# Seven places for gathered rows instead of four, and a quarter of the scratch for dynamic DMAs

## The chip, the core and the metric

The kernel runs on one core of a Trainium2 chip. The metric is the device time of one execution in microseconds (us). Before the change three runs took 2218.74, 2220.05 and 2222.28 us, with a median of 2220.05 us. The engines are named as in the profile: PE is TensorE (PEld its weight loads), DVE is VectorE, ACT is ScalarE, POOL is GpSimd, and SP is the queue that issues most plain DMAs.

## The reference, cut to what matters

Two transformer blocks run on a sequence of 512 tokens of width 1024, all in float32. The first block has attention with a sliding window, a convolution branch and a gated feed-forward layer. The second has a spatial gate, an attention over selected keys, and at its end a layer called PEER: each token picks 128 of 16,384 experts (8 heads, 16 each), and an expert is a row of two tables of 16,384 x 1024 numbers.

```python
def blk(args):                 # xb: 128 tokens, eb: 128 expert numbers of each, gb: their gates
    ub = u_tab[eb]
    vb = v_tab[eb]
    a = jax.nn.gelu(jnp.einsum('td,ted->te', xb, ub))
    return jnp.einsum('te,ted->td', (gb * a).astype(vb.dtype), vb)
```

## The kernel before

**Dense and gathered tokens.** The expert layer does most tokens densely. For the first 320 tokens PE multiplies with all 128 blocks of `peer_u` (`u_block`, 24 products of 128x320 each), and for the first 384 tokens with all 128 blocks of `peer_v` (`v_block`, 18 products of 128x512 each); what a token did not choose has weight zero. The other tokens use gathers: POOL issues an indirect DMA that fetches one row of 4 KB into each of 128 partitions (512 KB in all), and DVE multiplies. The generator `gathered()` holds the 320 gathers and their DVE instructions in this order: 64 from `peer_u` (for 64 tokens with 128 experts each, two experts of a token on two partitions; multiplied with `h[1]`, sums in `ga2`), 128 from `peer_u` (the last 128 tokens, multiplied with `h[3]`, sums in `ga`), and 128 from `peer_v` (added into `h[3]`).

**The ring.** All 320 go through one tile name with `GBUFS` buffers, which are the "places":

```python
def gather(table, idx, k):
    r = pg.tile([128, 1024], F32, name="rows", bufs=GBUFS)
    G.indirect_dma_start(out=r, out_offset=None, in_=table,
                         in_offset=bass.IndirectOffsetOnAxis(ap=idx[:, k:k + 1], axis=0))
    return r
# in gathered(), the last of its three loops:
        r = gather(A["peer_v"], gidx, k)
        with tc.issue_after(pace[0]):
            V.scalar_tensor_tensor(h[3], r, ga[:, k:k + 1], h[3], op0=OP.mult, op1=OP.add)
```

Gather k can be issued when the DVE instruction of gather k-4 has run. Weights have such rings too (`unit()`): four `raw` buffers that SP fills, and four each of `whi` (a cast by ACT, L137) and `wlo` (a subtraction by DVE, L139), which PE reads. A `raw` buffer is free again when its `wlo` has run.

**What sets the order.** Each engine runs its instructions in a fixed order. `advance(gen, us)` mixes the gathers among weight blocks by the costs that the generators yield (`G1_US`, `G_US`); a scheduler below then orders each engine's list, and `issue_after` keeps a gather's DVE instruction behind the `wlo` named by `pace`. Three stretches matter here:

- About 585 to 620 us: the norms on the way into the second block. DVE writes a scaled sum of squares, POOL turns it into `rstd` (L163), DVE scales `xs` (L174), PE transposes it. Soon after, the pool `b2g` is opened, which loads `vg`, `vb`, `wsT` and `bs` from ACT's queue (L93, L755, L760); POOL then masks `wsT` with four affine selects (L757).
- 1106 to about 1515 us: choice of experts and dense `peer_u` blocks. The first 64 gathers begin here. Where the program needs all of them (`while not made2: next(gat)`), those left over, 18 in the trace, follow each other; then ACT makes `zg` from `ga2`, PE multiplies it with `fold` (L1015), and building goes on.
- From there to the end: the 128 `v_block`s (the first product starts at 1516.9 us), with 28 of the `u_block`s among them, the other gathers, and loads of `gl` (gate weights, 1.5 MB for eight blocks) and `al` (stored `peer_u` results). A block's gate weights are multiplied by DVE (`gl`, L1164), cast by ACT (`wvhi`, L151), and split by DVE (`wvlo`, L152) before PE can start on it.

**The scratch.** [...] A place for gathered rows takes 4,096 bytes of each partition.

Of the kernel before, what the change touches and what calls it, by code (L numbers as in the profile page):

```python
# [19 lines left out]
DRAM = bass.MemoryType.DRAM  # L20
EPS = 1e-6
NEG = -1.0e30
GBUFS = 4

R_US = 2.1
TOP_US = 4.0
# [33 lines left out]
def tile_layers(ctx: ExitStack, tc: tile.TileContext, A: dict, out: bass.AP):  # L60
# [818 lines left out]
# [5 lines that stand above are left out]
# [446 lines left out]
```

## Time and profile before

| | before |
|---|---|
| median of 3 runs | 2220.05 us |
| the profiled execution, its own time | 2223.98 us |
| its span, first to last instruction | 2222.3 us |
| PE busy | 2082.0 us, 94% |
| DVE busy | 1583.9 us, 71% |
| ACT busy | 863.1 us, 39% |
| POOL busy | 501.1 us, 23% |
| moved by DMA | 476.47 MB |

The shares are means over stages with different limits. The line of GB/s in the profile shows the two halves: about 100 GB/s until 1100 us, and 290 to 373 GB/s from there until shortly before the end. [...] A wait is idle time of an engine and is put down to what ended it.

### The profile page before, as it was taken

The page shows a single profiled execution, that of the slowest core. Times are in us where ns is not written, and L with a number is a line of the kernel's source. Part 1 is how long each engine was busy: PE and PEld are TensorE (multiplying, and loading weights), DVE is VectorE, ACT ScalarE, POOL GpSimd, SP SyncE. Part 2 cuts the span into 40 slices and gives each one's busy share as a digit, 9 for nine tenths or more (in the row PEclk, how much of TensorE's full clock was granted, in tenths as well). Part 3 has the DMA queues.
Part 4 walks back from the last instruction along what each step waited for, and adds up shares of the span by engine and source line. Part 5 has one row for each costly group of instructions (what it writes and reads, how often), then busy time and mean ns, then how long its engine had stood idle before and what let it go on. Part 6 is the DMA issues. An engine that isn't in the chain of part 4 may idle for free.

```text
span 2222.3 us, 29478 instructions
## 1 busy us (share of the span) xinstructions
PE 2082.0 (94%) x11104; PEld 1767.1 (80%) x11104; DVE 1583.9 (71%) x2880; ACT 863.1 (39%) x1303; POOL 501.1 (23%) x383
## 2 busy tenths in 40 slices
PE   7989999999989999999999998899999899898889
PEld 6737888888777778888999997799787677777777
DVE  6984533332479654569999998887888788778873
ACT  4454422222344433333546765563333233232222
POOL 1000000000001000000031214323555556555550
PEclk9989999999999999999999999899999999999999
DMA  5202333333223213322688999999999999999992
GB/s 190 76 20 76 95 96 100 98 114 95 65 83 100 76 63 101 128 93 77 194 301 291 357 309 338 324 339 373 345 352 351 359 363 370 366 348 363 365 324 95
DMA packets 163281, 476.47 MB, mean 214 GB/s; under 512 B 13865, under 2 KB 57265, under 8 KB 161218
## 3 DMA queue, kind: packets, MB, share of 16 engines
q1 hardware_dynamic: 67104, 259.70, 34.1%
q0 software_dynamic: 46656, 169.18, 20.6%
q10 hardware_dynamic: 49378, 45.71, 6.2%
q8 instruction: 87, 1.43, 0.3%
q14 instruction: 56, 0.46, 0.1%
HBM read 432.18 MB, written 42.09 MB: 213 GB/s over the span
## 4 chain that ended last, share of the span: by engine, by line
PE 40%; issue 25%; DMA 14%; DVE 10%; POOL 9%; ACT 1%; POOLq 0%; DVEq 0%; SPq 0%; ACTq 0%
PE bank_a L155 9%; PE bank_a L156 9%; PE bank_a L157 9%; DMA rows<-in_peer_v_dram,gidx 9%; POOL rows L881 8%; PE bank_b L155 3%; PE bank_b L156 3%; PE bank_b L157 3%; DMA rows<-in_peer_u_dram,gidx 3%; DVE wlo L139 2%; DVE h L904 1%; PE bank_b L1048 1%; DVE rows L889 1%; POOL rstd L163 1%; DMA gl<-g_dram 1%
## 5 line engine op out<-in xcount | busy, mean ns | idle before, releaser
L137 ACT CAST whi<-raw 128x1024 fp32r<-128x1024 f32 (+1 forms) x413 | 432.1, 1047 | 851.1 <-PE bank_a L156 332.7
L139 DVE TENSOR_TENSOR wlo<-raw,whi 128x1024 fp32r<-128x1024 f32 (+1 forms) x413 | 500.4, 1214 | 268.2 <-ACT whi L137 265.9
L155 PE MATMUL bank_a<-xhi,whi 128*128 128x320 f32 (+2 forms) x1600 | 552.8, 346 | 9.4 <-ACT whi L137 8.4
L157 PE MATMUL bank_a<-xhi,wlo 128*128 128x320 f32 (+2 forms) x1600 | 546.9, 342 | 9.6 <-DVE wlo L139 9.6
L156 PE MATMUL bank_a<-xlo,whi 128*128 128x320 f32 (+2 forms) x1600 | 549.8, 344 | 0.6 <-DVE xlo L152 0.6
L881 POOL DMA_INDIRECT rows<-in_peer_u_dram,gidx x192 | 265.9, 1385 | 598.0 <-DVE rows L897 214.0
L155 PEld LDWEIGHTS bank_a<-xhi,whi 128*128 128x128 f32 x1600 | 304.9, 191 | 38.1 <-ACT whi L137 9.2
L157 PEld LDWEIGHTS bank_a<-xhi,wlo 128*128 128x128 f32 x1600 | 305.3, 191 | 36.0 <-DVE wlo L139 10.1
L156 PEld LDWEIGHTS bank_a<-xlo,whi 128*128 128x128 f32 x1600 | 305.8, 191 | 26.9 <-DVE xlo L152 1.6
L155 PE MATMUL bank_a<-whi,wvhi 128*128 128x512 f32 x512 | 209.9, 410 | 46.4 <-ACT wvhi L151 46.4
L881 POOL DMA_INDIRECT rows<-in_peer_v_dram,gidx x128 | 198.9, 1554 | 157.8 <-DVE h L904 136.3
L156 PE MATMUL bank_a<-wlo,wvhi 128*128 128x512 f32 x512 | 208.5, 407 | 3.1 <-DVE wlo L139 3.1
L163 POOL TENSOR_TENSOR rstd<-rstd,neghalf 128x1 f32<-128x1 f32 (+2 forms) x37 | 26.5, 718 | 818.9 <-DVE rstd L162 810.9
L157 PE MATMUL bank_a<-whi,wvlo 128*128 128x512 f32 x512 | 209.1, 408 | 1.5 <-DVE wvlo L152 1.5
L904 DVE SCALAR_TENSOR_TENSOR h<-rows,ga,h 128x1024 f32<-128x1024 f32 x128 | 164.2, 1283 | 60.1 <-DMA rows<-in_peer_v_dram,gidx 59.1
L897 DVE SCALAR_TENSOR_TENSOR rows<-rows,h 128x1024 f32<-128x1024 f32 x128 | 154.8, 1220 | 45.4 <-DMA rows<-in_peer_u_dram,gidx 45.1
L155 PEld LDWEIGHTS bank_a<-whi,wvhi 128*128 128x128 f32 x512 | 101.2, 198 | 70.2 <-ACT wvhi L151 50.7
L157 PEld LDWEIGHTS bank_a<-whi,wvlo 128*128 128x128 f32 x512 | 100.9, 197 | 29.5 <-DVE wvlo L152 8.4
L156 PEld LDWEIGHTS bank_a<-wlo,wvhi 128*128 128x128 f32 x512 | 101.5, 198 | 25.3 <-DVE wlo L139 5.0
L151 ACT CAST wvhi<-gl 128x768 fp32r<-128x768 f32 x56 | 45.6, 831 | 164.8 <-DVE gl L1164 98.1
L1049 ACT ACTIVATE gt<-bank_b 128x512 f32<-128x512 f32 x96 | 96.8, 1119 | 10.8 <-PE bank_b L1048 10.1
L155 PE MATMUL bank_b<-whi,wvhi 128*128 128x512 f32 x256 | 100.7, 393 | 0.0
(391 smaller groups left out, 3364.9 us busy)
## 6 DMA issues: line engine op xcount, KB each, us to landing
raw<-in_wt_dram SPq DMA_DIRECT2D x150, 512.0 KB
raw<-in_ut_dram SPq DMA_DIRECT2D x128, 512.0 KB
raw<-in_peer_v_dram SPq DMA_DIRECT2D x128, 512.0 KB
g_dram<-gt ACTq DMA_DIRECT2D x24, 896.0 KB
gl<-g_dram SPq DMA_DIRECT2D x14, 1536.0 KB
a_dram<-ab ACTq DMA_DIRECT2D x25, 640.0 KB
al<-a_dram SPq DMA_DIRECT2D x25, 640.0 KB
rows<-in_peer_u_dram,gidx POOLq DMA_INDIRECT x192
```

Source lines behind the costliest of these rows:

```text
L137: lead[0] = S.copy(hi[:, :n], raw[:, :n]).ins
L139: pace[0] = V.tensor_tensor(lo[:, :n], raw[:, :n], hi[:, :n].bitcast(F32), op=OP.subtract).ins
L151: a = S.copy(hi, src).ins
L155: T.matmul(o, lh, rh, start=start, stop=False)
L156: T.matmul(o, lh, rl, start=False, stop=False)
L157: T.matmul(o, ll, rh, start=False, stop=stop)
L163: G.tensor_tensor(r, r, neghalf[:, :shape[1]], op=OP.pow)
L881: G.indirect_dma_start(out=r, out_offset=None, in_=table, in_offset=bass.IndirectOffsetOnAxis(ap=idx[:, k:k + 1], axis=0))
L889: V.scalar_tensor_tensor(r, r, 1.0, hn2, op0=OP.mult, op1=OP.mult, accum_out=ga2[:, k:k + 1])
L897: V.scalar_tensor_tensor(r, r, 1.0, hn3, op0=OP.mult, op1=OP.mult, accum_out=ga[:, k:k + 1])
L904: V.scalar_tensor_tensor(h[3], r, ga[:, k:k + 1], h[3], op0=OP.mult, op1=OP.add)
L1049: S.activation(gt[:, :, t8 + 4 * q:t8 + 4 * q + 4].rearrange("p i t -> p t i"), gp, AF.Copy, scale=1.0 if made else 2.0 ** -14)
```

## The change

Two numbers change. `GBUFS` goes from 4 to 7, and the scratch of the dynamic DMAs from 16,384 to 4,096 bytes of each partition, so 12,288 bytes become free, which is what three places take.

```diff
-GBUFS = 4
+GBUFS = 7
+DMA_SCRATCH = 4096
...
-    nc = _bacc.Bacc("TRN2", target_bir_lowering=False, num_devices=1)
+    nc = _bacc.Bacc("TRN2", target_bir_lowering=False, num_devices=1, dynamic_dma_scratch_size=DMA_SCRATCH)
```

A line is added, so each line below it is numbered one higher after the change. What each engine executes stays the same. The order moves at two places. From 1530 us on no engine's order changes.

The first place is the load and mask of `wsT`. On ACT before, behind the copy of `idx0` out of PSUM:

```order
L151 CAST xhi_3394<-bank_b_4162 128x512
L634 COPY idx0_4337<-bank_a_4203 128x290
L668 ACTIVATE cn_4611,ssq1_4612<-idx0_4337 128x256
L634 COPY idx1_4338<-bank_a_4228 128x290
L172 ACTIVATE xs_4175,ssq_4179<-h3_73 128x1024
```

and after, in the same place:

```order
L152 CAST xhi_3394<-bank_b_4162 128x512
L635 COPY idx0_4337<-bank_a_4203 128x290
L756 DMA wsT_5177<-in_wsT_dram 128x512
L669 ACTIVATE cn_4611,ssq1_4612<-idx0_4337 128x256
L761 DMA bs_5183<-in_spatial_b_dram 1x512
```

The loads of `wsT` and `bs` came here from some 80 instructions further down; `vg` and `vb` came to the place just ahead of the two casts of `xhi`. On POOL, before, in the norms of the same stretch (`rstd_4181` belongs to `h[3]`, `rstd_4614` to `cn` of the first 128 tokens):

```order
L163 TENSOR_TENSOR rstd_4127<-rstd_4127,neghalf_77 128x1
L163 TENSOR_TENSOR rstd_4172<-rstd_4172,neghalf_77 128x1
L163 TENSOR_TENSOR rstd_4181<-rstd_4181,neghalf_77 128x1
L163 TENSOR_TENSOR rstd_4614<-rstd_4614,neghalf_77 128x1
L630 AFFINE_SELECT mask1_4327<-mask1_4327 128x128
```

and after:

```order
L164 TENSOR_TENSOR rstd_4127<-rstd_4127,neghalf_77 128x1
L164 TENSOR_TENSOR rstd_4172<-rstd_4172,neghalf_77 128x1
L758 AFFINE_SELECT wsT_5177<-wsT_5177 128x128 x4
L164 TENSOR_TENSOR rstd_4181<-rstd_4181,neghalf_77 128x1
L164 TENSOR_TENSOR rstd_4614<-rstd_4614,neghalf_77 128x1
```

The four selects stood twelve instructions further down, behind `rstd_5096`; now two norms stand behind them.

The second place is on DVE, in the 18 rows that follow each other (`rows_12025` to `rows_12076`; `oh1`, `oh2`, `ohh` are building work). Before, from the third of them:

```order
L889 SCALAR_TENSOR_TENSOR rows_12031,ga2_6475<-rows_12031,h1_71 128x1024
L889 SCALAR_TENSOR_TENSOR rows_12034,ga2_6475<-rows_12034,h1_71 128x1024
L139 TENSOR_TENSOR wlo_12100<-raw_12097,whi_12099 128x1024
L889 SCALAR_TENSOR_TENSOR rows_12037,ga2_6475<-rows_12037,h1_71 128x1024
L889 SCALAR_TENSOR_TENSOR rows_12040,ga2_6475<-rows_12040,h1_71 128x1024
L889 SCALAR_TENSOR_TENSOR rows_12043,ga2_6475<-rows_12043,h1_71 128x1024
L1034 TENSOR_TENSOR oh1_12130<-iota16_7081,sT2_7064 128x1024
L889 SCALAR_TENSOR_TENSOR rows_12046,ga2_6475<-rows_12046,h1_71 128x1024
```

and after, from the thirteenth:

```order
L890 SCALAR_TENSOR_TENSOR rows_12061,ga2_6475<-rows_12061,h1_71 128x1024
L890 SCALAR_TENSOR_TENSOR rows_12064,ga2_6475<-rows_12064,h1_71 128x1024
L890 SCALAR_TENSOR_TENSOR rows_12067,ga2_6475<-rows_12067,h1_71 128x1024
L140 TENSOR_TENSOR wlo_12100<-raw_12097,whi_12099 128x1024
L890 SCALAR_TENSOR_TENSOR rows_12070,ga2_6475<-rows_12070,h1_71 128x1024
L890 SCALAR_TENSOR_TENSOR rows_12073,ga2_6475<-rows_12073,h1_71 128x1024
L1035 TENSOR_TENSOR oh1_12130<-iota16_7081,sT2_7064 128x1024
L890 SCALAR_TENSOR_TENSOR rows_12076,ga2_6475<-rows_12076,h1_71 128x1024
```

`wlo_12100` stood behind the fourth row and stands behind the fifteenth now; the next one, `wlo_12164`, stood behind the twelfth and now follows all eighteen and three rows of the next loop. On PE the 24 products of one `u_block` move from ahead of the product with `fold` to behind it.

## Rows read from the trace of the kernel before

**Rows 1.** The page, the chain that ended last, shares by line.
```profile
PE bank_a L155 9%; PE bank_a L156 9%; PE bank_a L157 9%; DMA rows<-in_peer_v_dram,gidx 9%; POOL rows L881 8%; PE bank_b L155 3%; PE bank_b L156 3%; PE bank_b L157 3%; DMA rows<-in_peer_u_dram,gidx 3%; DVE wlo L139 2%; DVE h L904 1%; PE bank_b L1048 1%; DVE rows L889 1%; POOL rstd L163 1%; DMA gl<-g_dram 1%
```
**Rows 2.** Windows: length; PE, PEld, DVE, ACT, POOL busy; clock, DMA share, GB/s.
```profile
1530.00:2168.00 638.00, 580.04 (x2601) 481.73 (x2600) 526.59 (x585) 194.06 (x220) 345.26 (x226) 0.94 0.96 357
2168.00:2222.00 54.00, 50.33 (x212) 41.05 (x211) 20.62 (x21) 10.86 (x12) 0.00 (x0) 0.94 0.29 98
2050.00:2100.00 50.00, 43.12 (x206) 36.53 (x205) 40.43 (x38) 12.92 (x15) 25.19 (x17) 0.98 0.99 384
1990.00:1995.00 5.00, 5.00 (x24) 4.14 (x23) 0.71 (x1) 1.05 (x1) 0.36 (x1) 1.00 1.00 410
2010.00:2015.00 5.00, 5.00 (x24) 4.13 (x23) 5.00 (x6) 0.00 (x0) 3.69 (x3) 1.00 0.79 275
```
**Rows 3.** Waits of DVE, 1530 to 2168 us: in total, times, longest.
```profile
DVE h L904 <- DMA rows<-in_peer_v_dram,gidx: 59.1, 44, 5.1
DVE rows L897 <- DMA rows<-in_peer_u_dram,gidx: 44.2, 33, 3.3
DVE gl L1164 <- DMA al<-a_dram: 8.0, 3, 4.8
DVE wvlo L152 <- ACT wvhi L151: 0.2, 1, 0.2
```
**Rows 4.** Waits of PE, 1530 to 2168 us, the longest.
```profile
PE bank_a L155 <- ACT wvhi L151: 46.4, 10, 6.9
```
**Rows 5.** Waits of ACT, 1530 to 2168 us: those for gate weights and for weights.
```profile
ACT wvhi L151 <- DVE gl L1164: 98.1, 11, 11.2
ACT whi L137 <- DMA raw<-in_peer_v_dram: 77.4, 28, 9.0
ACT whi L137 <- DMA raw<-in_ut_dram: 28.4, 6, 7.0
```
**Rows 6.** Timeline of SP, POOL and DVE at 1982 to 1995 us: start, length.
```profile
1982.62 0.33 SPq L1161 DMA_DIRECT2D gl<-g_dram  x1
...
1989.42 0.94 POOL L881 DMA_INDIRECT rows<-in_peer_v_dram,gidx  x1 [1.35 <-DVE h L904]
...
1994.29 1.28 DVE L904 SCALAR_TENSOR_TENSOR h<-rows,ga,h 128x1024 f32<-128x1024 f32 x1 [5.14 <-DMA rows<-in_peer_v_dram,gidx]
```
**Rows 7.** Timeline of DVE in the 18 rows that follow each other.
```profile
1364.80 1.23 DVE L889 SCALAR_TENSOR_TENSOR rows<-rows,h 128x1024 f32<-128x1024 f32 x1 [1.50 <-DMA rows<-in_peer_u_dram,gidx]
...
1390.76 1.22 DVE L889 SCALAR_TENSOR_TENSOR rows<-rows,h 128x1024 f32<-128x1024 f32 x1 [2.81 <-DMA rows<-in_peer_u_dram,gidx]
```
**Rows 8.** Timeline of PE there: nine lines of L156 make 24 products, then two waits.
```profile
1364.69 0.31 PE L156 MATMUL bank_a<-xlo,whi 128*128 128x320 f32 x1
...
1368.21 0.31 PE L156 MATMUL bank_a<-xlo,whi 128*128 128x320 f32 x1
...
1383.97 0.63 PE L157 MATMUL bank_a<-xhi,wlo 128*128 128x320 f32 x1 [9.43 <-DVE wlo L139]
...
1396.20 0.66 PE L1015 MATMUL bank_b<-fold,zg 128*128 128x64 f32 x2 [3.65 <-issue]
```
**Rows 9.** Timeline of ACT, POOL and PE: copy, norms and transposes, the load of wsT.
```profile
609.76 0.41 ACT L634 COPY idx<-bank_a 128x290 f32<-128x290 f32 x1
...
614.89 1.06 POOL L163 TENSOR_TENSOR rstd<-rstd,neghalf 128x1 f32<-128x1 f32 x2 [5.41 <-DVE rstd L162]
616.90 1.06 PE L182 MATMUL bank_b<-cst,xs 128*128 128x128 f32 x8 [1.31 <-DVE xs L174]
...
705.90 0.45 ACTq L755 DMA_DIRECT2D wsT<-in_wsT_dram  x1
...
712.83 1.03 POOL L757 TENSOR_SCALAR_AFFINE_SELECT wsT<-wsT 128x128 f32<-128x128 f32 x4 [12.20 <-DMA wsT<-in_wsT_dram]
```
**Rows 10.** Timeline of POOL, the longest issue of a gather.
```profile
2139.12 3.90 POOL L881 DMA_INDIRECT rows<-in_peer_v_dram,gidx  x1 [0.30 <-issue]
```

## The prediction

> **What bounds the kernel now.** I read the chain that ended last first. It has two entries that belong to the gathers' data, `rows<-in_peer_v_dram` with 9% and `rows<-in_peer_u_dram` with 3%, and POOL's issues of them with 8% [rows 1]: a fifth of the chain hangs on gathers, so their ring is no side matter. Then I read the windows, to see where in the program that is. From 1530 to 2168 us no engine is full (PE 580 of 638 us, DVE 527), but the DMA engines are busy 96% of the time at 357 GB/s; from 2168 us on, when the last gather is consumed, DMA is nearly idle (0.29) and PE runs the rest alone [rows 2]. That last piece of 54 us has no gather in it and stays as it is.
>
> The waits of DVE come next. Its idle time in the 638 us is 59.1 + 44.2 us for gathered rows, 8.0 us for `al`, and next to nothing else [rows 3]; with 526.6 us busy that makes 638.1. So in this stretch DVE either works or waits for DMA, nearly always for a row, 77 times. It works in order, so what stands behind a waiting row is late too: the gate product `gl`, for which ACT waits 98.1 us in 11 waits [rows 5], and for the cast behind it PE waits 46.4 us in 10 waits [rows 4]. This is how a late row costs PE time. [...]
>
> One such event in the timeline: SP issues `gl` (1.5 MB) at 1982.62, a gather is issued at 1989.42, and DVE stands 5.14 us until 1994.29 [rows 6]. In the 5 us of that wait DMA runs at 410 GB/s with share 1.00. Twenty us later, while DVE works without a gap, its share is only 0.79 at 275 GB/s [rows 2]. So demand comes in turns: when DVE is the limit, all four places are filled and nothing more may be fetched; when a large load comes, the four rows in hand are soon used up.
>
> **The change, part by part.** The sum is made against the profiled execution's own 2223.98 us (span 2222.3), which is 3.9 us above the median of 2220.05.
>
> *Three more places from 1530 to 2168 us.* The instructions and their order are the same; gather k waits for row k-7 rather than k-4. The 226 gathers there (the count of POOL's instructions [rows 2]) take 226 x 0.524 MB = 118 MB of 638 us x 357 GB/s = 228 MB. DVE takes a row each 638 / 226 = 2.8 us, so a gather may start 3 x 2.8 = 8.5 us earlier, longer than the longest wait for a row, 5.1 us [rows 3]. If DMA were free, all 103.3 us of row waits would go. It is not: the same 228 MB must move. The idle part of DMA is 4% of 638 us = 26 us, which is what better filling gives if a share of 1.00 is the end. The best 50 us ran at 384 GB/s with share 0.99 [rows 2]; at that rate the bytes take 228 / 0.384 = 593 us, a gain of 45 us. The other end is 0. I take three quarters of the 26 us, **-20 us**: three rows are only 1.6 MB, about 4 us of DMA at full rate, as large as one `gl` load but not as two demands on top of each other, so not each idle slice gets filled. What is late next is then the weights, on the same DMA engines. Cover for the loss: PE has 58 us of idle time, more than 20, and DVE 112.
>
> *The 18 rows in a row.* Here DVE runs faster than the rows land: from the fifth, at 1364.80, to the sixteenth, at 1390.76, eleven rows take 25.96 us, 2.36 us each [rows 7]. With seven in stock instead of four each later row is met three landings earlier, so the eighteenth, and with it `zg` and the product with `fold` at 1396.20, comes 3 x 2.36 = 7.1 us earlier. Against this stands the moved `wlo_12100`: one `u_block` of PE's work less ahead of that product. Between its nine shown lines lie 24 products in 1368.21 - 1364.69 = 3.5 us [rows 8]; PE idles for that and does them later. The sum is **-3.5 us**, between -7 (if the block is hidden later) and +3.5 (if the rows land no earlier). PE waits 9.43 and 3.65 us there [rows 8], so there is room for it.
>
> *The early load of `wsT`.* This is the price. POOL works in order, and the four selects now stand ahead of the norm of `h[3]`. Before, from the issue of the load at 705.90 to the selects at 712.83 it takes 6.9 us, and the selects 1.03 [rows 9]. Now it is issued behind the copy of `idx0`, which ends at 609.76 + 0.41 = 610.2; it lands at 617.1 and the norm can start at 618.2 rather than 614.89: 3.3 us late. Behind it wait DVE's `xs` and PE's transposes, which already waited 1.31 us at 616.90 [rows 9], so nothing covers it. If the load lands sooner, as `vg` and `vb` no longer go out in the same microsecond, it costs less, and nothing if it lands by 613.6. I take **+2 us**, between 0 and 3.3. What the move saves at 705 us is ACT's and POOL's time, and PE does not wait for either there: 0.
>
> *The smaller scratch.* [...] A gather's issue takes 1.5 us on the mean (345.26 / 226 [rows 2]), 0.94 in the row at 1989.42, and 3.90 at most [rows 6, 10]. The end below is 0, as nothing gets shorter by less room. The end above: should each of the 226 take 3.90 + 0.30 us, POOL needs 949 us, 311 more than the stretch has. Seven gathers are fewer than twice the four in flight today, so I take 0; POOL's 293 idle us in the stretch cover a fifth of the gathers at 3.90 several times over.
>
> Sum: -20 - 3.5 + 2 = **-21.5 us**, 2223.98 - 21.5 = 2202.5 us for that execution, and 2198.5 us against the median.
>
> **The rivals.**
>
> *DMA is at its ceiling* and the wait only changes its name: rows land in time, weights don't. For it: share 0.96. Against it: 384 GB/s over 50 us. It gives 0 for the first part and -1.5 with the others, 2218.5 us. [...]
>
> *DMA fills better than I take*, up to the 384 GB/s: -45 - 1.5 = -46.5, 2173.5 us. For it: 410 GB/s in the row above, with both kinds of traffic waiting. Against it: that mean is one piece of 50 us out of 638, and the whole has 357.
>
> *Slower: the weights starve.* Four `raw` buffers now share the DMA engines with seven gathers. In the stretch ACT waited for a weight 28 + 6 = 34 times, 105.8 us [rows 5]. If each is 3 x 0.524 MB / 357 GB/s = 4.4 us later, that makes 150 us of new lateness against 103 us of row waits. It decides from 103 / 150 = 69% on: if three quarters reach DVE, 112 - 103 = +9, with the rest 2227.5 us. Against it: DVE never once waits for a cast weight here [rows 3], so there is slack between ACT and DVE, and DVE's order keeps the ratio of rows to weights.
>
> *Slower: POOL becomes the bound*, by the scratch or because DVE stands still less. It decides when an issue with its gap takes over 638 / 226 = 2.8 us; with a fifth more than that, 3.4 us, the stretch grows by 130 us, to 2350. For it: 0.94 us with DVE waiting, 3.90 with DVE working [rows 6, 10]. [...]
>
> **How the numbers follow.** My forecast has 0.58, the better filling 0.16, the ceiling 0.13, the starving weights 0.10, POOL 0.03. A measurement of this kernel tells 0.2%, 4.4 us, from no change. So faster has 0.58 + 0.16 = 0.74, and the same goes to the ceiling, 0.13; slower has 0.10 + 0.03 = 0.13. The range reaches down to the 384 GB/s, 2174, and up past the ceiling case, with a little for the two small parts at their worse ends, to 2224; beyond lie POOL, most of the starving, and little else.
>
> **What would show it.** DVE's waits for rows from 103 us to under 50 in the last stretch; DMA share there 0.98 or more and over 365 GB/s; the last row consumed at about 2146 us rather than 2168, with the same 54 us behind it; PE's waits for `wvhi` halved. The product with `fold` 3 to 7 us earlier against the start of its 18 rows. POOL's norm behind the selects near 617 us. POOL's issues at 1.5 us on the mean, and none long at even distances. I am wrong if row waits shrink and waits for `raw` grow as much, or if rows wait as before while POOL's issues are long.

## The result, and the profile after

The changed kernel takes **2143.58 us** (median of 4 runs, 2142.29 to 2144.38) where the kernel before takes 2219.39 (4 runs beside it, 2213.83 to 2222.28): a ratio of 0.966, 95% interval 0.964 to 0.968. That is 76 us faster; 21.5 were forecast, and the time lies below the range. The profiled execution took 2144.32 us, its span 2142.6.

The direction and most of the signs were right; the size of one term was wrong by more than a factor of three. The chain that ended last shows where. In [rows 1] it hangs on rows of peer_v, POOL's gathers and rows of peer_u with 9, 8 and 3%; now with 6, 4 and 2%:

```profile
PE bank_a L158 6%; DMA rows<-in_peer_v_dram,gidx 6%; PE bank_a L156 6%; PE bank_a L157 6%; POOL rows L882 4%; PE bank_b L156 3%; PE bank_b L157 3%; PE bank_b L158 3%; DVE wlo L140 2%; DMA rows<-in_peer_u_dram,gidx 2%; DVE rows L898 1%; DVE h L905 1%; PE bank_b L1049 1%; DVE rows L890 1%; DMA gl<-g_dram 1%
```

(Lines of the changed kernel are one higher than those of before.) The last loop, from the same first to the same last product, in windows of each kernel: length, then busy us (and instructions) of PE, PEld, DVE, ACT, POOL, then clock, DMA share, GB/s. Before:

```profile
1516.90:2218.30 701.40, 643.44 (x2881) 534.43 (x2880) 557.04 (x619) 210.63 (x238) 351.13 (x230) 0.95 0.91 338
```

After, and below it the last 50 us without gathers, which answer to the 54 us of [rows 2]:

```profile
1514.00:2139.00 625.00, 612.92 (x2882) 517.62 (x2880) 553.53 (x620) 211.64 (x238) 363.38 (x227) 0.99 0.95 377
2092.00:2142.00 50.00, 46.71 (x207) 38.34 (x205) 19.75 (x20) 10.67 (x12) 0.00 (x0) 1.00 0.32 106
```

The loop is 76.4 us shorter, as much as the whole kernel. The same products keep PE busy 30.5 us less (643.44 - 612.92), at a granted clock of 0.99 of full speed instead of 0.95, and PE idles 45.9 us less (58.0 before, 12.1 now). So PE stops much less, and its granted clock, which reads 1.00 or 0.50 in both traces, is at 0.50 for 6.8 us of the loop instead of 75.1 (worked out from the two traces). (The last piece without gathers, forecast to stay as it is, became 4 us shorter, at a clock of 1.00 instead of 0.94.) DVE's waits from 1526 to 2092 us (in total, times, longest) show what had held it up; 103.3 us for rows in [rows 3] are 13.5 now:

```profile
DVE gl L1165 <- DMA al<-a_dram: 15.8, 5, 4.6
DVE h L905 <- DMA rows<-in_peer_v_dram,gidx: 10.6, 12, 1.9
DVE gl L1165 <- DMA gl<-g_dram: 6.8, 3, 3.0
DVE wlo L140 <- ACT whi L138: 6.1, 7, 1.6
DVE rows L898 <- DMA rows<-in_peer_u_dram,gidx: 2.9, 4, 1.3
```

PE's 46.4 us of waits for `wvhi` [rows 4] became 9.6, and ACT's waits for the gate product fell from 98.1 to 41.8 while those for weights of peer_v fell too, from 77.4 to 61.1 [rows 5]. Waits of PE and of ACT in the same stretch:

```profile
PE bank_a L156 <- ACT wvhi L152: 9.6, 4, 4.5
...
ACT whi L138 <- DMA raw<-in_peer_v_dram: 61.1, 19, 9.3
ACT wvhi L152 <- DVE gl L1165: 41.8, 11, 6.4
```

The other two places moved as forecast, and one of them cost more. In the 18 rows that follow each other the last one starts 29.7 us behind the first (36.8 before), 7.0 us earlier. But PE now waits 14.21 us for a weight there instead of 9.43 [rows 8]. The product with `fold` comes 3.8 us earlier in absolute time, and 6.2 us earlier against the first of the 18 rows, which starts 2.4 us later than before.

POOL's norm stands behind the four selects. POOL and PE there, answering to [rows 9], where the norm began at 614.89 and PE's transposes at 616.90 behind a wait of 1.31 us:

```profile
617.11 1.03 POOL L758 TENSOR_SCALAR_AFFINE_SELECT wsT<-wsT 128x128 f32<-128x128 f32 x4 [7.28 <-DMA wsT<-in_wsT_dram]
618.11 1.07 POOL L164 TENSOR_TENSOR rstd<-rstd,neghalf 128x1 f32<-128x1 f32 x2
...
620.13 1.07 PE L183 MATMUL bank_b<-cst,xs 128*128 128x128 f32 x8 [4.19 <-DVE xs L175]
```

The norm ahead of it had begun 0.35 us later than before (608.59 against 608.24), so the move costs the norm 2.9 us. By POOL's next select, which waits for PE, it has grown to 4.6 us, that is 4.3 us by the move. This line is from before and the next one from after:

```profile
634.77 0.29 POOL L630 TENSOR_SCALAR_AFFINE_SELECT mask<-mask 128x128 f32<-128x128 f32 x1 [18.82 <-PE bank_a L157]
639.40 0.29 POOL L631 TENSOR_SCALAR_AFFINE_SELECT mask<-mask 128x128 f32<-128x128 f32 x1 [20.22 <-PE bank_a L158]
```

### The profile page after: what moved, and what is told of

It is laid out like the page before. It is cut to its first block, busy times and chain, and to the rows that moved or that the text cites. A ratio compares the mean times of both kernels' runs of the same rounds, so it can differ in the third digit from the quotient of the medians.

```text
span 2142.6 us, 29429 instructions
## 1 busy us (share of the span) xinstructions
PE 2046.9 (96%) x11104; PEld 1745.5 (81%) x11104; DVE 1579.6 (74%) x2880; ACT 863.4 (40%) x1303; POOL 518.8 (24%) x383
## 4 chain that ended last, share of the span: by engine, by line
PE 28%; issue 20%; DVE 9%; DMA 9%; POOL 4%; ACT 0%; POOLq 0%; DVEq 0%; SPq 0%; ACTq 0%
PE bank_a L158 6%; DMA rows<-in_peer_v_dram,gidx 6%; PE bank_a L156 6%; PE bank_a L157 6%; POOL rows L882 4%; PE bank_b L156 3%; PE bank_b L157 3%; PE bank_b L158 3%; DVE wlo L140 2%; DMA rows<-in_peer_u_dram,gidx 2%; DVE rows L898 1%; DVE h L905 1%; PE bank_b L1049 1%; DVE rows L890 1%; DMA gl<-g_dram 1%
## 5 line engine op out<-in xcount | busy, mean ns | idle before, releaser
L156 PE MATMUL bank_a<-xhi,whi 128*128 128x320 f32 (+2 forms) x1600 | 549.8, 345 | 4.4 <-ACT ab L878 2.1
L882 POOL DMA_INDIRECT rows<-in_peer_u_dram,gidx x192 | 279.7, 1457 | 541.9 <-DVE gidx L983 167.0
L156 PEld LDWEIGHTS bank_a<-xhi,whi 128*128 128x128 f32 x1600 | 302.5, 189 | 32.7 <-ACT ab L878 2.4
L882 POOL DMA_INDIRECT rows<-in_peer_v_dram,gidx x128 | 202.7, 1584 | 111.3 <-DVE h L905 94.3
L156 PE MATMUL bank_a<-whi,wvhi 128*128 128x512 f32 x512 | 200.8, 392 | 9.6 <-ACT wvhi L152 9.6
L158 PE MATMUL bank_a<-whi,wvlo 128*128 128x512 f32 x512 | 200.8, 392 | 1.9 <-DVE wvlo L153 1.9
L157 PE MATMUL bank_a<-wlo,wvhi 128*128 128x512 f32 x512 | 200.2, 391 | 0.3 <-DVE wlo L140 0.3
L156 PEld LDWEIGHTS bank_a<-whi,wvhi 128*128 128x128 f32 x512 | 96.7, 189 | 30.1 <-ACT wvhi L152 11.3
L158 PEld LDWEIGHTS bank_a<-whi,wvlo 128*128 128x128 f32 x512 | 96.5, 188 | 24.8 <-DVE wvlo L153 4.8
L157 PEld LDWEIGHTS bank_a<-wlo,wvhi 128*128 128x128 f32 x512 | 96.7, 189 | 19.9 <-DVE wlo L140 0.6
L157 PE MATMUL bank_b<-wlo,wvhi 128*128 128x512 f32 x256 | 99.6, 389 | 0.0
L158 PE MATMUL bank_b<-whi,wvlo 128*128 128x512 f32 x256 | 99.6, 389 | 0.0
```

The lines of the kernel that those rows point to most:

```text
L156: T.matmul(o, lh, rh, start=start, stop=False)
L157: T.matmul(o, lh, rl, start=False, stop=False)
L158: T.matmul(o, ll, rh, start=False, stop=stop)
L882: G.indirect_dma_start(out=r, out_offset=None, in_=table, in_offset=bass.IndirectOffsetOnAxis(ap=idx[:, k:k + 1], axis=0))
```

## The experiments

Three theories. **L, lead:** a place gives its row so much time to land as the other places last, and with four that is too little; DVE works in order, so a late row holds up gate products and casts, and PE idles and loses clock. **Q:** any more bytes in flight make DMA faster, whose they are doesn't matter. **S:** the smaller scratch itself speeds gathers. Beside them **C**, the step of the prediction: DMA was at its end, a share of 1.00 being that end.

Ratios are against the kernel before on the same chip, with 95% intervals. The last two columns are worked out from DVE's waits from 1526 us on and from windows over 1700 to 2000 us.

| places for rows | us | ratio | DVE's waits for rows, us | share, GB/s |
|---|---|---|---|---|
| 3, small scratch | 2304.82 | 1.039 [1.036, 1.042] | 182.6 (111) | 0.90, 326 |
| 4, small scratch | 2221.05 | 1.0015 [0.9998, 1.0032] | 103.4 (79) | 0.96, 365 |
| 5 | 2165.79 | 0.976 [0.974, 0.978] | 44.1 (40) | 1.00, 394 |
| 6 | 2149.40 | 0.969 [0.968, 0.971] | 28.8 (31) | 1.02, 402 |
| 7 (the change) | 2143.58 | 0.966 [0.964, 0.968] | 13.5 (16) | 1.02, 406 |

**The small scratch alone.**

```diff
-GBUFS = 7
+GBUFS = 4
 DMA_SCRATCH = 4096
```

> Four places, but the small scratch (4096 bytes), so the early load of wsT is in it as well. Theory L (lead: with four places rows come too late for an in-order DVE, and PE idles and cools behind it): nothing but the wsT price of some 3 us, 2222 us (2217 to 2227), and DVE's waits for rows in the last stretch near 100 us as before. Theory S (the smaller ring itself speeds gathers): most of the gain without any place, 2150 to 2175 us. Theory Q (any further transfer in flight lifts the DMA rate): as L, 2222 us, since none is added.

2221.05 us, ratio 1.0015 [0.9998, 1.0032]. L holds and S is out: without the places nothing is gained. This kernel also has the early load of `wsT`, since the smaller scratch is what moves it; by the upper end of the interval its price over the whole kernel can be no more than some 7 us.

**Five places, and six.**

```diff
-GBUFS = 7
-DMA_SCRATCH = 4096
+GBUFS = 5            # the other run: 6
+DMA_SCRATCH = 12288  # the other run: 8192
```

> Five places, scratch 12288 bytes. L: a row may start 2.8 us earlier, where the waits of before are 1.34 us on the mean (103.3 us in 77) and 5.1 at the longest, so the first place takes about half of the gain: 2180 us (2165 to 2195), row waits 40 to 65 us. A ceiling in steps (all three places are needed before the casts come in time): 2205 to 2215 us. S, in proportion to the room given up (4 of 12 KB): about 2195 us.

> Six places, scratch 8192 bytes. L: less is left with each place, 2157 us (2148 to 2168), row waits 20 to 35 us, PE over 97% busy in the last stretch at a granted clock of 0.97 or more. In steps: 2190 us or more. S: about 2170 us.

2165.79 and 2149.40 us. Places and scratch take 32,768 bytes of each partition together in both, as in the changed kernel; beside four places that makes a scratch of 16,384. The fifth place alone gives 55 us against the small scratch, the sixth 16, the seventh 6. Both lie in L's ranges, near their fast ends, and the row waits of 44.1 and 28.8 us lie in L's ranges too. DVE's waits for rows with five places:

```profile
DVE h L905 <- DMA rows<-in_peer_v_dram,gidx: 27.6, 25, 4.2
DVE rows L898 <- DMA rows<-in_peer_u_dram,gidx: 16.5, 15, 2.6
```

And the window from 1700 to 2000 us:

```profile
1700.00:2000.00 300.00, 284.64 (x1300) 237.41 (x1299) 269.70 (x285) 97.75 (x111) 183.89 (x119) 0.97 1.00 394
```

Here the share already reads 1.00, and two more places still raise the rate by 12 GB/s, in the changed kernel's window:

```profile
1700.00:2000.00 300.00, 291.95 (x1357) 245.47 (x1355) 277.79 (x288) 102.94 (x116) 194.23 (x123) 0.99 1.02 406
```

A share of 1.00 is not the end of DMA, and C is out.

**Three more buffers for weights instead.**

```diff
-GBUFS = 7
+GBUFS = 4
-        raw = ring.tile([128, 1024], F32, tag="raw", name="raw", bufs=4)
+        raw = ring.tile([128, 1024], F32, tag="raw", name="raw", bufs=7)
```

> Four places for rows, but seven instead of four buffers for raw weights in the same room (scratch 4096 bytes): as many bytes may be in flight as in the changed kernel. L: the rows wait as before, since their lead over DVE is the same; the weights come from further ahead and take nothing off DVE's waits: 2219 us (2205 to 2228), row waits 90 to 115 us. Q: the rate of DMA rises as in the changed kernel, 2145 to 2165 us.

2208.92 us, ratio 0.997 [0.995, 0.999]. Room for as many bytes in flight gives 6 us by the ratio (2 to 10), of 77. The median is 12 us below that of the small scratch alone, but that is no price of the buffers: with seven of them the load of `wsT` goes out late again, and POOL's selects follow at 711.74 us, so this kernel doesn't pay for the early load. The buffers were used: ACT's waits for weights, 105.8 us before [rows 5], are gone but for one of 2.3 us. The rate from 1700 to 2000 us is 362 GB/s all the same (365 with the small scratch alone), so Q is out. The row waits stand nearly as before:

```profile
DVE h L905 <- DMA rows<-in_peer_v_dram,gidx: 59.1, 41, 4.5
DVE rows L898 <- DMA rows<-in_peer_u_dram,gidx: 40.0, 32, 3.7
```

**Half of each row of peer_v, with seven places and with four.**

```diff
-            r = gather(A["peer_v"], gidx, k)
+            r = pg.tile([128, 1024], F32, name="rows", bufs=GBUFS)
+            G.indirect_dma_start(out=r[:, 0:512], out_offset=None, in_=A["half"], ...)
...
-                V.scalar_tensor_tensor(h[3], r, ga[:, k:k + 1], h[3], ...)
+                V.scalar_tensor_tensor(h[3].rearrange("p (a n) -> p a n", a=2), r[:, None, 0:512].to_broadcast([128, 2, 512]),
+                                       ga[:, k:k + 1], h[3].rearrange("p (a n) -> p a n", a=2), ...)
...
+    A["half"] = np.ascontiguousarray(I["peer_v_2"][0][:, 0:512])
```

This kernel leaves out the other half of each row. The run with four places has `GBUFS = 4` besides.

> Seven places; each of the 128 rows of peer_v is fetched to half (512 of its 1024 numbers; the other half is left out, DVE reads the fetched half twice, so its work keeps its length). 33.5 MB less for DMA, as many gathers, rows and instructions. L: with seven places DMA no longer sets the pace, PE does (12 us idle in 566); little changes: 2140 us (2134 to 2145), while DMA's rate in the last part falls under 370 GB/s. Rival C (DMA is still at its end, at some 400 GB/s, and everything waits for bytes): 33.5 MB at 400 GB/s are 84 us, of which PE's idle time and lost clock let some 18 through: 2125 us.

> The same half rows of peer_v with four places (and the small scratch). L: a row is late because it lands later than the lead of its place; with half the bytes it lands sooner, so the 58 us of waits for rows of peer_v fall to about 20, the 45 us for peer_u stay: 2221 - 40 = 2181 us (2168 to 2195). Rival C, the theory of the prediction (DMA at its end before, a share of 1.00 being the ceiling): 33.5 MB at 357 GB/s are 94 us, so the stretch falls to where PE stops it, 2140 to 2150 us, and the waits for peer_u fall too. No effect at all (2215 to 2225) would mean that the landing time does not hang on a row's bytes.

With four places 2182.58 us, ratio 0.985 [0.983, 0.987]: L's 2181, not C's 2140 to 2150. DVE's waits for rows:

```profile
DVE rows L898 <- DMA rows<-in_peer_u_dram,gidx: 44.8, 30, 5.8
DVE h L907 <- DMA rows<-in_half_dram,gidx: 21.5, 13, 2.5
```

The waits for the half rows fell from 58.1 to 21.5 us. Those for the whole rows of peer_u stayed at 45, but that tells nothing of C: DVE reads the last row of peer_u at 1810 us and the first of peer_v at 1814, so nothing was taken from the stretch in which peer_u's rows are late. The stretch of peer_v's rows is the one to compare. Here it is with four places (small scratch) and whole rows, with four places and half rows, and in the changed kernel:

```profile
1817.40:2168.30 350.90, 314.89 (x1420) 260.77 (x1419) 295.75 (x269) 105.83 (x119) 185.56 (x124) 0.95 0.95 358
1813.66:2127.30 313.64, 306.66 (x1429) 257.67 (x1428) 293.50 (x269) 106.60 (x120) 200.49 (x124) 0.99 0.85 296
1777.70:2091.90 314.20, 306.96 (x1438) 258.79 (x1437) 294.74 (x269) 108.14 (x121) 192.27 (x123) 0.99 1.01 402
```

Half the bytes give there what three more places give with all of them: 37 us. L expects that, as a smaller row lands sooner; C expects it too, as fewer bytes have to pass. C's number was too low because it let the gain go past this stretch. So the run fits L but doesn't part it from C; the five and seven places did that.

With seven places 2133.71 us, ratio 0.963 [0.961, 0.965]; between L and C, 10 us below the changed kernel by the medians, 7 by the ratios. From 1700 to 2000 us:

```profile
1700.00:2000.00 300.00, 295.71 (x1376) 249.56 (x1375) 286.45 (x295) 104.90 (x118) 203.45 (x127) 0.99 0.92 337
```

PE's idle time there falls from 8.0 to 4.3 us, and in the stretch of peer_v's rows alone PE is busy without a gap, 301.6 us instead of 314.2. So the changed kernel is nearly PE's, but not wholly: some ten microseconds still hang on transfers. L's 2140 was too strict.

**The load of wsT put back behind the norm**, by 12 KB of unused room that restores its old address.

```diff
     wk = pool("b2g", stack=stw)
+    wk.tile([128, 3072], F32, name="pad")
```

> The changed kernel with 12 KB of unused room ahead in the pool of wsT, so that wsT lies where it lay before, and its load and POOL's four selects go out some 95 us later again, behind the norm. The term of the prediction (+2, read now as 2.9 us at PE's transposes): 2143.6 - 3 = 2140.6 us (2139 to 2142.5). Rival (PE's later start there is made up behind, since other work waits for other things): within 1 us of the changed kernel.

2138.27 us, ratio 0.9655 [0.9637, 0.9673]. By the medians 5.3 us less than the changed kernel, by the ratios 1.3, with intervals that overlap. POOL does the norm first again:

```profile
614.42 1.07 POOL L164 TENSOR_TENSOR rstd<-rstd,neghalf 128x1 f32<-128x1 f32 x2 [5.41 <-DVE rstd L163]
...
712.13 1.04 POOL L759 TENSOR_SCALAR_AFFINE_SELECT wsT<-wsT 128x128 f32<-128x128 f32 x4 [11.97 <-DMA wsT<-in_wsT_dram]
```

The norm is 3.7 us earlier than in the changed kernel (618.11 against 614.42), but 0.8 of that stood already at the norm ahead of it (608.59 against 607.77), so 2.9 are the move's; POOL's select that waits for PE comes at 634.30 instead of 639.40. What of it reaches the end these runs can't tell more finely than 1 to 5 us.

**More rows beside the early u_blocks.**

```diff
-G1_US = 0.9
+G1_US = 1.25
```

> The changed kernel with more gathered rows beside each of the 100 early u_blocks (G1_US 1.25 for 0.9), so that no 15 rows are left in a row ahead of the fold product, where PE stands for 14.2 and 2.2 us and runs at 0.74 of its clock in 1360 to 1400 us. If those rows find room beside the u_blocks: 2143.6 - 12 = 2132 us (2126 to 2138). Rival (DVE, 95% busy from 1100 to 1360 us, has no room, and 18 rows of 1.2 us push the casts of the weights back): 2143 us or up to 2155.

2130.06 us, ratio 0.962 [0.960, 0.964], 13.5 us below the changed kernel by the medians, 10 by the ratios. PE is busy for all of 1360 to 1400 us, at a clock of 1.00:

```profile
1360.00:1400.00 40.00, 40.00 (x343) 38.70 (x341) 40.00 (x67) 29.11 (x44) 12.27 (x10) 1.00 1.05 381
```

The same window of the changed kernel:

```profile
1360.00:1400.00 40.00, 22.17 (x148) 20.81 (x147) 31.84 (x57) 13.23 (x21) 28.55 (x21) 0.74 0.99 360
```

So the rows in a row leave PE idle for 17.8 of these 40 us in the changed kernel, and cost clock besides (0.74). In the same window of before PE idles 16.9 us: the three places bring the last row sooner, but leave this hole.

**Both, then the rows spread to the end, then that with four places.**

```diff
+    wk.tile([128, 3072], F32, name="pad")
-G1_US = 0.9
+G1_US = 1.25
-G_US = 2.4
+G_US = 2.2       # not in the first of the three
-GBUFS = 7
+GBUFS = 4        # in the last of the three alone
```

> The changed kernel with both edits that helped by themselves: wsT where it lay before (-5.3 us) and G1_US 1.25 (-13.5 us). They lie in different stages (600 and 1360 us), so they add: 2143.6 - 18.8 = 2125 us (2121 to 2129). If one only hides the other: 2130 us.

> As the run before, and G_US 2.2 for 2.4, which spreads the rows of the last loop to its end instead of leaving its last blocks without any. L, with seven places: rows already come in time and PE is the bound, so nothing: within 3 us of the run before. If the loop still waits for DMA's rate: 5 to 12 us faster.

> All edits of the run before, with four places again (small scratch kept). L: four places give a row every 2.8 us whatever the plan asks; spreading the rows helps only by the 50 us at the end, in which none is asked for now. 192 rows of the last loop at 2.84 us are 545 us, so the loop may end near PE's pace: 2150 to 2190 us, taken as 2170. If places matter for themselves (the rate of DMA, as in Q): 2200 us or more.

Both edits: 2125.34 us, ratio 0.959 [0.957, 0.961]; they add as expected. Spread rows: **2114.50 us**, ratio 0.955 [0.952, 0.957], the best of all and 10.8 us below the run before on the same chip. L expected nothing there and missed; as with the half rows, some 10 us were still to be had from the loop's transfers. In the spread kernel the rate from 1700 to 2000 us is a little lower than the 411 GB/s of the run before it, and PE is busier (297.32 against 293.50 us):

```profile
1700.00:2000.00 300.00, 297.32 (x1404) 252.49 (x1403) 270.12 (x270) 102.80 (x116) 183.36 (x113) 0.99 1.01 402
```

With four places 2160.26 us, ratio 0.975 [0.972, 0.978]. Of the 103 us between the kernel before (2217.47 us beside these runs) and the best, a better plan of the rows takes 57 without any place; the three places are worth 46 on top of it, and 76 without it.

**Three places.**

```diff
-GBUFS = 7
+GBUFS = 3
```

> Three places, small scratch, all else as before. L by the turn of a place (issue 1.5, landing some 6 to 7.5, DVE 1.2, gap 0.6 us: 9.3 to 10.8 us for each place): a row every 3.1 to 3.6 us instead of 2.84, so 226 rows are 60 to 170 us longer: 2221 + 95 = 2316 us (2280 to 2390), row waits in the last stretch over 160 us, PE's clock there under 0.92. Rival C (DMA at its end with four places already): with three places its share stays at 0.95 or more and the time grows by under 30 us.

2304.82 us, in L's range and outside C's. DVE waits 182.6 us for rows, and the share falls to 0.90:

```profile
DVE h L905 <- DMA rows<-in_peer_v_dram,gidx: 99.6, 59, 5.4
DVE rows L898 <- DMA rows<-in_peer_u_dram,gidx: 83.0, 52, 5.2
```

```profile
1700.00:2000.00 300.00, 253.95 (x1080) 207.14 (x1081) 221.60 (x253) 81.28 (x92) 143.19 (x97) 0.91 0.90 326
```

Taking one place away lowers the rate by 39 GB/s (365 to 326) and costs 84 us, so with three the places set the pace. By itself this would still allow an end of DMA that is reached at four; that the rate goes on rising with five, six and seven rules it out.

## Why the prediction was wrong

**Three more places from 1530 to 2168 us: the mis-sized term.** It stood at -20 us with bounds of 0 and -45. The loop measured -76.4; over the whole kernel, seven places are 77.5 us faster than four with the same small scratch. The step that failed is "The idle part of DMA is 4% of 638 us = 26 us, which is what better filling gives if a share of 1.00 is the end". The share counts the time that packets took, and a packet's time is no fixed price of its bytes. Before, the loop's packets took 0.91 x 701.4 = 638 us for 338 GB/s x 701.4 us = 237 MB; after, 0.95 x 625.0 = 594 us for 236 MB. Nearly the same bytes took 44 us less of that "busy" time, which the sum had held constant. So a share of 0.96 said that a transfer was nearly always on its way, not that no more could be. The prediction's own rows spoke against it: 410 GB/s at a share of 1.00 and 384 at 0.99 [rows 2] would be some 370 to 395 at 0.96 if a byte always took the same time, and the stretch had 357.

What should have been asked is how long the places leave a row to land. The k-th gather belongs to the k-th row that DVE reads, so both can be put together. POOL of before issues one at 1982.00:

```profile
1982.00 1.41 POOL L881 DMA_INDIRECT rows<-in_peer_v_dram,gidx  x1 [0.65 <-DVE h L904]
```

It is the row at 1994.29 in [rows 6]: 12.3 us from issue to landing, with a `gl` load between. Over the last loop, as worked out from all such pairs, it is 9.4 us from a gather's issue to DVE's read of its row, 1.3 us of reading, and some 0.3 till the place's next issue: 11 us for one turn of a place, and with four places a row each 2.76 us (230 rows). That this is the pace of the rows proves nothing by itself: a place is issued again when its row was read, so turn and pace go together whatever the bound is, and with seven places it is 7 x 2.44 = 17.1 us. And most rows were in time: DVE waited for 77 of 226 [rows 3].

The question is what the places leave at the pace that the loop could have. At the 2.44 us of the changed kernel, as an estimate, four places leave a row 4 x 2.44 - 1.5 - 1.3 - 0.3 = 6.7 us to land behind its issue of 1.5 us, and seven leave 14.0. One of the gathers with seven places, and its row:

```profile
1905.06 1.27 POOL L882 DMA_INDIRECT rows<-in_peer_v_dram,gidx  x1 [2.53 <-DVE h L905]
...
1919.08 1.28 DVE L905 SCALAR_TENSOR_TENSOR h<-rows,ga,h 128x1024 f32<-128x1024 f32 x1 [0.59 <-DMA rows<-in_peer_v_dram,gidx]
```

From its issue on it took 14.0 us to land and cost DVE a wait of 0.59. Of the rows that DVE waited for, and these are the late ones, the landing, from the end of the issue, took 7.6 us on the mean with four places (small scratch), 11.5 with six and 12.8 with seven: more in flight makes each slower, by 5.2 us from four places to seven, but the room grows by 7.3, so fewer come late and the rate rises. The prediction had the 8.5 us of extra lead and the 103 us of waits, and the experiments show them to be the right terms: from three places to seven the time falls by 161.2 us and the row waits by 169.1. It then cut them down to a DMA ceiling that was not there.

The same term had a second lack. The clock of 0.94 stood in [rows 2] and was not priced. PE's busy time fell by 30.5 us for the same products, as its clock rose from 0.95 to 0.99 and it stood less. The only cover named on PE was its 58 us of idle time, of which 45.9 went; the busy time gave two thirds as much again.

**The bound of -45 us** was the best 50 us of before, 384 GB/s. In the 5 us of a full wait the rate was 410 [rows 2], and the changed kernel holds 406 for 300 us. The short stretch with everything in flight was the better bound, and the text had set it aside as a turn of demand.

**The 18 rows in a row:** forecast 7.1 us earlier for the last row, measured 7.0. In absolute time 3.8 us are left at the product with `fold`, close to the -3.5 taken, but partly by luck: the rows began 2.4 us late, and against the first of them the product comes 6.2 us earlier, with the moved `u_block` (3.5 us [rows 8]) still to be done behind it. What was not seen is the size of the hole that stayed: 10 to 13.5 us more by planning the rows otherwise.

**The early load of wsT:** forecast to land at 617.1 with the norm at 618.2; measured 617.11 and 618.11. That it fits so closely is partly luck, as all of this stretch ran 0.35 us later than before. The term was too small: the norm is 2.9 us late by the move and what follows on POOL and PE 4.3 us, where 2 were taken and 3.3 was the end of the range. Why it grows between the two was not followed. For the end of the kernel the runs tell only 1 to 5. **The smaller scratch:** 0 taken, on the author's estimate, as no run shows how much of the scratch a gather takes. Nothing in the run with it alone speaks for more than the move of `wsT`, and POOL's longest issue in the changed kernel is 3.5 us (3.90 before [rows 10]).

**The rivals.** DMA at its ceiling: out, with 406 GB/s for 300 us against a mean of 357. DMA fills better: right in kind, and it should have had the higher chance. Starving weights: out, ACT's waits for weights of peer_v fell from 77.4 to 61.1 us; that there is "slack between ACT and DVE" is borne out by the seven `raw` buffers, which took nearly all of ACT's waits for weights away and left DVE's waits for rows at 99.1 us. POOL: out; it issued 227 gathers in 363 of 625 us, 1.60 us each with DVE 89% busy, and 230 in 351 of 701 us before, 1.53 us each with DVE 79% busy.

Of the signs that the prediction named these came out: row waits under 50 us, share over 0.98 in the windows inside the loop, the waits for `wvhi` more than halved, the product with `fold` 3 to 7 us earlier against the start of its rows. The last row's end, 2092 us instead of 2146, did not.

Open stays why a packet takes less time when more are in flight. In the packets of gathered rows from 1700 to 2000 us, as worked out from the two traces, the median is 159 ns before and 160 after, and the mean 173 and 164; the slowest hundredth took over 512 ns before and over 174 after. So it is a few long packets that went, but nothing here separates the engines' own work from the memory's. How the 76 us part into idle time and clock is read from the two traces and was not tried by itself.

## What to carry to other kernels

- For a ring of places work out what it leaves a transfer to land: the places times the pace wanted, less issue, use and release. Compare that with the landings of the late ones, and look at the waits of the in-order engine that reads the ring; the DMA share doesn't tell it. Up to the sixth place the time fell here by about as much as those waits (55 and 16 us against 59 and 15), and the seventh gave 6 us for 15.
- A DMA share near 1.00 was no ceiling here. The better bound on the rate was a short stretch in which everything waits for DMA: 410 GB/s in 5 us of before, and 406 for 300 us after.
- When a stall in front of PE goes, price the lost clock as well as the idle time. Here PE idled 45.9 us less and was busy 30.5 us less for the same products, with the clock at 0.99 instead of 0.95.

## What was not expected of the hardware

- The DMA share reads up to 1.05 (1360 to 1400 us with the rows planned otherwise), and at a reading of 0.99 or 1.00 the rate can be 384, 394 or 410 GB/s.
- The DMA engines of one core moved 411 GB/s for 300 us (1700 to 2000 us of the kernel with both edits).
- Seven gathers of 512 KB in flight did well with a scratch of 4096 bytes: the issue took 1.6 us on the mean for rows of peer_v (202.7 us for 128), 3.5 at most.
